# One layer of a hybrid diffusion trunk: the gated output weights prepared earlier and kept in scratch, the router's column sums moved, eight weight splits on another engine

## The chip, the cores and the metric

The kernel runs on one core of a Trainium2 chip. Its engines run side by side and each works through its own queue in order: TensorE (PE for matmuls, PEld for the loading of their weights), VectorE (DVE), ScalarE (ACT), GpSimd (POOL) and SyncE (SP), which here only starts transfers. ACT and POOL start transfers too. Sixteen DMA engines carry them all between the chip's main memory and SBUF, the memory on the core. The metric is the device time of one execution in microseconds (us), as the median of the runs.

## The reference

One layer with 2048 latent tokens and 256 context tokens of width 1024. Four token mixers of width 256 (HGRN2, gated DeltaNet, a grouped Fourier transform, Mamba-2 SSD) read the normed input `hl`. Their outputs are merged and projected, and a mixture of 16 experts follows:

```python
def merge_branches(h, outs, w_gate, b_gate, w_branch, w_out):
    t = [jax.nn.sigmoid(h @ w_gate[g] + b_gate[g]) * (outs[g].astype(h.dtype) @ w_branch[g])
         for g in range(N_BRANCH)]
    return (t[0] + t[1] + t[2] + t[3]) @ w_out

xl = post_norm(DEEPNORM_ALPHA * xl + g1_l * y_l, ln1_g[l], ln1_b[l])
hl2 = modulate(xl, sh2_l, sc2_l)
xl = post_norm(DEEPNORM_ALPHA * xl + g2_l * expert_choice_ffn(hl2, w_router[l], ...), ln2_g[l], ln2_b[l])
```

`g1_l`, `sh2_l`, `sc2_l` and `g2_l` are rows of 1024 numbers worked out from the conditioning vector. The router computes softmax(`hl2 @ w_router`), and each expert takes the 256 tokens that like it most.

## The kernel before, in words

A matmul in float32 is made of three in a shorter format: `split` (lines 105 to 108) makes a high part `hi` with a cast on ACT and a low part `lo` with a subtraction, on DVE or, where `eng` says so, on POOL. `mm3` (lines 110 to 117) then issues high x high (line 115), high x low (116) and low x high (117). So L106 is always the cast, L108 the subtraction and L115 to L117 the three matmuls, and the names of the tiles tell which work it is.

The stages in order of time: projections of the input (to about 800 us), gated DeltaNet (its chain ends with `finish`, whose last store of `d_oB` goes out at 1519.7 us), HGRN, which takes its four heads one after the other from inside the DeltaNet stretch to 1726 us, SSD, the Fourier mixer (to 2068 us), the merge, routing (about 2570 to 2650 us) and the experts (to the end). From 800 to 2143 us TensorE also works through `gates`, the products of the input with `w_gate`: 2 groups of tokens by 32 blocks of 128 columns. The framework's planner puts them between the other stages' matmuls when it fixes every engine's order at compile time, by the order of the program and its own estimates. On the chip that order doesn't change: an engine whose next instruction has to wait stands still. A tile with `bufs=n` has n buffers in turn, and the load into the next one waits in its queue until that buffer is free.

HGRN (`hgrn`, lines 829 to 939) loads its inputs from POOL's queue. After heads 1 and 3 it calls `finish` (lines 941 to 962): sums of squares, a normalisation, then four times a load of 512 columns of a gate (`fns`, one buffer, from SP, line 959), two DVE operations (960, 961) and a store from SP (962). `hoT`, the tile that is finished, has one buffer, so head 2 may write its outputs (line 936) only once all four stores of head 0 and 1 have landed.

The merge works on groups of 512 tokens in the order 2, 3, 0, 1. `branch` (lines 1644 to 1678) does one mixer n of one group i: it loads the mixer's output `bo` and splits it, gets the weights `bwh` and `bwl` for each pair of 128-column blocks, does six matmuls for each block, and DVE multiplies the result by the gate `bt` that it loads from `d_th` (1674, 1676); the sum into `t` (1677) is on DVE for group 2 and on POOL for the others. The weights come from `w_branch` through a split for all four mixers of group 2 and for the last two (n = 2, 3) of group 3; that split's subtraction is on POOL. The first two mixers' parts go to the scratch `d_wbs` in group 2 and the last two's in group 3, from ACT's queue (1663); the other passes read them back from SP (1666). Group 2's `branch` runs beside the last blocks of `gates`.

`combine` (lines 1685 to 1710) starts with `out_weights`, four calls of two blocks each: it loads the row g1 (`oa`), then each of the 8 blocks `ox` (128x1024, three buffers) of `w_out`, multiplies it by 0.5 g1 on DVE (1724) and splits it into `owh` and `owl`. The first call also loads and scales the router's weights (`router_weights`: 128 values of `wrt`, and `wrc`, a transfer of 2048 single numbers), the last one loads four rows of 1024 and calls `router_sums`, which sums the router's columns on DVE (1749), adds them over the partitions with a matmul (1750) and copies the result (1751). Then group 3's `branch` alternates with `out_proj` of the group before: four tiles of 128 tokens, each a split of `t` into `oth`, `otl`, 48 matmuls, two layer norms on DVE with a square root on ACT (`rst`, L288), and stores; and with `logits`, eight transposes, a copy by ACT (`oxT`, L1802) and eight small matmuls (1805).

Of the kernel before, what the change touches and what calls it, by code (L numbers as in the profile page):

```python
# [9 lines left out]
F32 = mybir.dt.float32  # L10
F32R = mybir.dt.float32r
# [4 lines left out]
OP = mybir.AluOpType  # L16
# [3 lines left out]
D = 1024  # L20
NB = D // 128
SEQ = 2048
CTX = 256
TOT = CTX + SEQ
W = 256
# [17 lines left out]
def ap(t, offset, dims):  # L43
    return bass.AP(tensor=t.tensor, offset=t.offset + offset, ap=[list(d) for d in dims])


class Kernel:
# [522 lines left out]
    def front(self):  # L570
        nc, tc = self.nc, self.tc
        self.pos_c = self.const([128, D // 2], F32, "pos_c")
        for j in range(2):
            nc.sync.dma_start(self.pos_c[j * 64:(j + 1) * 64], self.a["pos_cc"])
        with tc.tile_pool(name="wp", bufs=1, reuse_waits="tile") as self.wp, tc.tile_pool(name="mc", bufs=1) as self.cpool:
            with tc.tile_pool(name="hp", bufs=1, reuse_waits="tile") as self.hp:
                with tc.tile_pool(name="ha", bufs=1, reuse_waits="tile") as hap, self.psum(4, 4):
                    self.stage_z(hap)
                with self.psum(3, 3):
                    with tc.tile_pool(name="hg", bufs=1, reuse_waits="tile") as p:  # L580
                        self.head_sel(p)
                        with tc.tile_pool(name="g3", bufs=1, reuse_waits="tile") as q:
                            self.gdn_merge(q)
                        with tc.tile_pool(name="g4", bufs=1, reuse_waits="tile") as q:
                            self.gdn_chain(q, p)
                        sp = tc.tile_pool(name="sp", bufs=1, reuse_waits="tile", side="right")
                        spp = sp.__enter__()
                        self.hgrn(p)
                        self.ssd_early(spp)
                    with tc.tile_pool(name="mp", bufs=1, reuse_waits="tile") as p:  # L590
                        self.ssd(p)
                    sp.__exit__(None, None, None)
                    with tc.tile_pool(name="mp", bufs=1, reuse_waits="tile") as p:
                        self.fourier(p)
                    self.cq = tc.tile_pool(name="cq", bufs=1, reuse_waits="tile", side="right")
                    self.cp = self.cq.__enter__()
                    self.merged = self.cp.tile([128, NB, 512], F32, name="t", bufs=2)
                    first = chain.from_iterable(self.branch(self.cp, 2, n, self.merged) for n in range(4))
                    self.gates(first)
                    for _ in first:  # L600
                        pass
            self.cpool = self.cn
# [338 lines left out]
    def finish(self, p, o, b, norm, gate, out, eps=EPS):  # L941

        nc = self.nc
        w = p.tile([128, 1], F32, name="fnw", bufs=2)
        nc.sync.dma_start(w, ap(self.a[norm], 128 * b, [[1, 128], [1, 1]]), allow_slow_non_contiguous=True)

        def tmp():
            return p.tile([128, 512], F32, name="fns", bufs=1)

        def sq(_, c, n):  # L950
            q = tmp()
            nc.scalar.activation(q, o[:, c:c + n], AF.Square)
            return q
        rs = self.head_rs(p, sq, [[(c, 512) for c in range(0, SEQ, 512)]], 1.0 / 64, self.hind, eps)
        rs = self.head_parts(p, rs)
        for g in range(4):
            s = slice(g * 512, g * 512 + 512)
            gt = tmp()
            nc.sync.dma_start(gt, ap(self.dram(gate, (W, SEQ)), 128 * b * SEQ + g * 512, [[SEQ, 128], [1, 512]]))
            nc.vector.tensor_mul(o[:, s], o[:, s], self.head_bc(rs, 4 * g, 512))  # L960
            nc.vector.scalar_tensor_tensor(o[:, s], o[:, s], w, gt, op0=OP.mult, op1=OP.mult)
            nc.sync.dma_start(ap(self.dram(out, (W, SEQ)), 128 * b * SEQ + g * 512, [[SEQ, 128], [1, 512]]), o[:, s])

# [678 lines left out]
    def branch(self, p, i, n, acc):  # L1644

        nc = self.nc
        g, name = ((2, "oC"), (3, "oD"), (0, "oA"), (1, "oB"))[n]
        o = p.tile([128, 2, 512], F32, name="bo", bufs=1)
# [5 lines left out]
        for b in range(NB):  # L1654
            if b % 2 == 0:
                wh, wl = [p.tile([128, 2, 256], F32R, name="bw" + s, bufs=3) for s in "hl"]
                parts = [(t.rearrange("p k c -> p (k c)").bitcast(F32), kept[j, 4 * g + b // 2]) for j, t in enumerate((wh, wl))]
                if i == 2 or i == 3 and n > 1:
                    wr = p.tile([128, 2, 256], F32, name="bw", bufs=3)
                    nc.sync.dma_start(wr, ap(self.a["w_branch"], g * W * D + b * 128, [[D, 128], [128 * D, 2], [1, 256]]))  # L1660
                    self.split(wr, wh, wl, nc.gpsimd)
                    for t, k in parts if i == 3 or n < 2 else ():
                        nc.scalar.dma_start(k, t)
                else:
                    for t, k in parts:
                        nc.sync.dma_start(t, k)
            ps = self.big()
            s = slice(b % 2 * 128, b % 2 * 128 + 128)
# [16 lines left out]
    def combine(self, p, op, rc):  # L1685

        nc = self.nc
        self.op = op
        for n in range(4):
            self.out_weights(op, n)  # L1690
        old, last = self.merged, 2
        xs = []

# [3 lines left out]
        for i in (3, 0, 1):  # L1697
            t = p.tile([128, NB, 512], F32, name="t", bufs=2)
# [10 lines left out]
            route()  # L1709
        self.logits(p, *xs[0])  # L1710

    def out_weights(self, p, n):

        nc = self.nc
        modr = self.dram("modr", (4, D))
        if n == 0:
            self.g1 = p.tile([128, D], F32, name="oa", bufs=1)
            nc.sync.dma_start(self.g1, ap(modr, 0, [[0, 128], [1, D]]))
            self.router_weights(p)
            self.wo = [p.tile([128, NB, D], F32R, name="ow" + s) for s in "hl"]  # L1720
        for k in (2 * n, 2 * n + 1):
            r = p.tile([128, D], F32, name="ox", bufs=3)
            nc.sync.dma_start(r, ap(self.a["w_out"], k * 128 * D, [[D, 128], [1, D]]))
            nc.vector.scalar_tensor_tensor(r, r, 0.5, self.g1, op0=OP.mult, op1=OP.mult)
            self.split(r, self.wo[0][:, k], self.wo[1][:, k])
        if n == 3:
            self.rowt = [self.row_tile(p, n, t, o) for n, t, o in (("sh2", modr, D), ("sc2", modr, 2 * D),
                                                                   ("lg", self.a["ln1_g"], 0), ("lb", self.a["ln1_b"], 0))]
            self.router_sums(p)

    def router_weights(self, p):

# [568 lines left out]
```

## Time and profile before

| | us |
|---|---|
| median of 3 runs | 3817.27 (3816.72 to 3832.19) |
| the profiled execution | 3813.39 |
| its span, first to last instruction | 3811.4 |
| TensorE busy in the span | 3516.1 |

The mean granted TensorE clock is 0.957 of full speed. In the slices of the span TensorE is nearly full in the experts' stage (2650 to 3550 us) and mostly between 8 and 10 tenths before it. The lowest slices are around the start of `combine` (2150 to 2200 us) and in routing (2550 to 2650 us). Times below are microseconds from the span's start unless marked ns; in a row of a timeline the first number is the start, the second the length, and the bracket tells how long the engine was idle before and what ended it.

### The profile page before, as it was taken

To read this page: it belongs to the slowest core of one execution; us is meant where nothing else is said; L and a number is where in the kernel's file an instruction comes from. 1 tells how busy PE (TensorE), PEld (TensorE's weight loads), DVE (VectorE), ACT (ScalarE), POOL (GpSimd) and SP (SyncE) were. 2 spreads that over 40 slices of the span, in tenths; PEclk is the share of its full clock that TensorE was granted. 3 is DMA by queue.
4 is the path that set the end of the run, shared out by engine and by line. 5 is a ranking of instruction groups with operands and counts; after the bars stand their busy time and mean duration, and the time that the engine had idled before them with its cause. 6 is when DMAs were issued, how large, how long until landed. Compare 5 with 4: busy or idle time off the path is not lost. (4 is left out here: it accounts for less than half of the span.)

```text
span 3811.4 us, 60074 instructions
## 1 busy us (share of the span) xinstructions
PE 3516.1 (92%) x23429; PEld 2939.9 (77%) x23429; DVE 2399.4 (63%) x4455; ACT 1222.9 (32%) x1863; POOL 785.0 (21%) x577
## 2 busy tenths in 40 slices
PE   5999999999888999898899789994999999999997
PEld 3897778777666667677777677873999999999887
DVE  6528762257557778567864666776555555555788
ACT  3513232212334223232234211112444444444342
POOL 2100013321222111214422254453101001001011
PEclk8999999999899999898999989996999999999999
DMA  7544438764656566424456787743666666657786
GB/s 237 166 143 133 145 96 196 182 170 130 154 123 152 169 186 200 124 66 138 135 172 216 237 272 233 252 149 134 205 206 199 220 209 212 217 193 222 270 274 206
DMA packets 602061, 699.81 MB, mean 184 GB/s; under 512 B 153809, under 2 KB 460465, under 8 KB 598577
## 3 DMA queue, kind: packets, MB, share of 16 engines
q1 hardware_dynamic: 537776, 547.56, 46.9%
q0 software_dynamic: 24800, 90.71, 8.9%
q10 hardware_dynamic: 39200, 57.69, 4.3%
q8 instruction: 185, 3.03, 0.3%
q14 instruction: 100, 0.81, 0.1%
HBM read 525.37 MB, written 170.45 MB: 183 GB/s over the span
## 5 line engine op out<-in xcount | busy, mean ns | idle before, releaser
L115 PE MATMUL big<-h2h,whi 128*128 128x512 f32 x704 | 292.5, 416 | 4.6 <-ACT ev L1595 4.6
L115 PE MATMUL mx<-exh,wgateh 128*128 128x256 f32 x1024 | 294.9, 288 | 0.0
L117 PE MATMUL big<-h2h,wlo 128*128 128x512 f32 x704 | 291.8, 415 | 1.4 <-POOL wlo L108 1.4
L116 PE MATMUL big<-h2l,whi 128*128 128x512 f32 x704 | 291.1, 413 | 0.0
L116 PE MATMUL mx<-exl,wgateh 128*128 128x256 f32 x1024 | 289.8, 283 | 0.0
L116 PE MATMUL mx<-exl,wuph 128*128 128x256 f32 x1024 | 289.8, 283 | 0.0
L115 PE MATMUL mx<-exh,wuph 128*128 128x256 f32 x1024 | 289.8, 283 | 0.0
L117 PE MATMUL mx<-exh,wupl 128*128 128x256 f32 x1024 | 289.8, 283 | 0.0
L117 PE MATMUL mx<-exh,wgatel 128*128 128x256 f32 x1024 | 289.8, 283 | 0.0
L116 PE MATMUL big<-h3l,whi 128*128 128x512 f32 x704 | 287.6, 408 | 0.0
L115 PE MATMUL big<-h3h,whi 128*128 128x512 f32 x704 | 287.5, 408 | 0.0
L117 PE MATMUL big<-h3h,wlo 128*128 128x512 f32 x704 | 286.1, 406 | 0.0
L108 POOL TENSOR_TENSOR wlo<-wraw,whi 128x1024 fp32r<-128x1024 f32 x60 | 147.4, 2457 | 643.0 <-ACT whi L106 611.7
L2126 POOL DMA_INDIRECT d_acc<-ey,ix x30 | 52.2, 1739 | 874.7 <-DVE ey L2119 837.4
L117 PE MATMUL big<-wdh,hidl 128*128 128x512 f32 x496 | 195.1, 393 | 10.5 <-DVE hidl L108 10.5
L108 DVE TENSOR_TENSOR wdl<-wdr,wdh 128x1024 fp32r<-128x1024 f32 x124 | 150.9, 1217 | 82.4 <-ACT wdh L106 82.3
L116 PEld LDWEIGHTS mx<-exl,wgateh 128*128 128x128 f32 x1024 | 196.3, 192 | 2.7 <-DVE exl L108 0.3
L115 PEld LDWEIGHTS mx<-exh,wgateh 128*128 128x128 f32 x1024 | 196.1, 192 | 2.4
L116 PEld LDWEIGHTS mx<-exl,wuph 128*128 128x128 f32 x1024 | 196.6, 192 | 0.0
L117 PEld LDWEIGHTS mx<-exh,wupl 128*128 128x128 f32 x1024 | 196.6, 192 | 0.0
L115 PEld LDWEIGHTS mx<-exh,wuph 128*128 128x128 f32 x1024 | 196.6, 192 | 0.0
L115 PE MATMUL big<-wdh,hidh 128*128 128x512 f32 x496 | 196.0, 395 | 0.2 <-ACT hidh L106 0.2
(642 smaller groups left out, 9127.4 us busy)
## 6 DMA issues: line engine op xcount, KB each, us to landing
wgr<-in_w_ff_gate_dram SPq DMA_DIRECT2D x64, 1024.0 KB
wgr<-in_w_ff_up_dram SPq DMA_DIRECT2D x64, 1024.0 KB
wdr<-in_w_ff_down_dram SPq DMA_DIRECT2D x128, 512.0 KB
wraw<-in_w_gate_dram POOLq DMA_DIRECT2D x64, 512.0 KB, 5.1
d_th<-ev ACTq DMA_DIRECT2D x128, 256.0 KB
bt<-d_th SPq DMA_DIRECT2D x128, 256.0 KB
adr<-in_ada_w_dram SPq DMA_DIRECT2D x128, 128.0 KB
bwh<-d_wbs SPq DMA_DIRECT2D x40, 256.0 KB
```

The source lines that it names most:

```text
L108: return (eng or self.nc.vector).tensor_tensor(lo, src, hi, op=OP.subtract)
L115: self.nc.tensor.matmul(ps, wh, xh, start=first and k == 0, stop=False)
L116: self.nc.tensor.matmul(ps, wh, xl, start=False, stop=False)
L117: self.at_pe = self.nc.tensor.matmul(ps, wl, xh, start=False, stop=last and k == n - 1).ins
L2126: nc.gpsimd.indirect_dma_start(out=acc, out_offset=bass.IndirectOffsetOnAxis(ap=ix[e][:, k:k + 1], axis=0), in_=weighted(e, k), in_offset= ...
```

## The change

Six edits in one.

- `scaled_out`, new, runs between DeltaNet and HGRN in the program's order: it loads the row g1 in two halves and `w_out` in 16 pieces of 128x512, multiplies each by 0.5 g1 on DVE and stores it to a new scratch `d_wos`. `issue_after(self.fin)` puts its transfers behind the last store of DeltaNet's `finish` in SP's queue; `finish` now keeps that store in `self.fin`. Its tiles have two buffers (`wor`) and one (`wog`).
- `out_weights` loads the 8 blocks from `d_wos` and only splits them; the row `oa` and the multiplication are gone.
- `router_weights` and `router_sums` are called ahead of group 2's `branch` and the last blocks of `gates`, in the pool of the merge.
- In `branch` the subtraction of the weights' split goes to DVE in group 3; in group 2 it stays on POOL.
- The four calls of `out_weights` are one.
- The memory kept for POOL's DMA descriptors is set to 8192 bytes.

```diff
                             self.gdn_chain(q, p)
+                        with tc.issue_after(self.fin):
+                            self.scaled_out()
...
                     self.cp = self.cq.__enter__()
+                    self.router_weights(self.cp)
+                    self.router_sums(self.cp)
                     self.merged = self.cp.tile([128, NB, 512], F32, name="t", bufs=2)
...
-                    self.split(wr, wh, wl, nc.gpsimd)
+                    self.split(wr, wh, wl, nc.gpsimd if i == 2 else None)
...
-        for n in range(4):
-            self.out_weights(op, n)
+        self.out_weights(op)
...
+    def scaled_out(self):
+        nc, p = self.nc, self.wp
+        wos = self.dram("wos", (D, D))
+        for j in range(2):
+            g = p.tile([128, 512], F32, name="wog", bufs=1)
+            nc.sync.dma_start(g, ap(self.dram("modr", (4, D)), j * 512, [[0, 128], [1, 512]]))
+            for k in range(NB):
+                r = p.tile([128, 512], F32, name="wor", bufs=2)
+                at = k * 128 * D + j * 512, [[D, 128], [1, 512]]
+                nc.sync.dma_start(r, ap(self.a["w_out"], *at))
+                nc.vector.scalar_tensor_tensor(r, r, 0.5, g, op0=OP.mult, op1=OP.mult)
+                nc.sync.dma_start(ap(wos, *at), r)
...
+    def out_weights(self, p):
...
+        for k in range(NB):
             r = p.tile([128, D], F32, name="ox", bufs=3)
-            nc.sync.dma_start(r, ap(self.a["w_out"], k * 128 * D, [[D, 128], [1, D]]))
-            nc.vector.scalar_tensor_tensor(r, r, 0.5, self.g1, op0=OP.mult, op1=OP.mult)
+            nc.sync.dma_start(r, ap(wos, k * 128 * D, [[D, 128], [1, D]]))
             self.split(r, self.wo[0][:, k], self.wo[1][:, k])
...
-    nc = bacc.Bacc("TRN2", target_bir_lowering=False, num_devices=1)
+    nc = bacc.Bacc("TRN2", target_bir_lowering=False, num_devices=1, dynamic_dma_scratch_size=8192)
```

## Rows read from the trace of the kernel before

**Rows 1.** The page's first part: busy us (share of the span) xinstructions of each engine.
```profile
PE 3516.1 (92%) x23429; PEld 2939.9 (77%) x23429; DVE 2399.4 (63%) x4455; ACT 1222.9 (32%) x1863; POOL 785.0 (21%) x577
```

**Rows 2.** Windows: stretch, length, busy us of each engine (xinstructions), TensorE's clock, DMA share, GB/s.
```profile
2150.00:2200.00 50.00, 26.50 (x97) 18.72 (x96) 45.82 (x59) 13.29 (x15) 6.66 (x5) 0.80 0.85 264
```

**Rows 3.** Timeline of TensorE, 2173 to 2200 us.
```profile
2187.54 0.64 PE L1750 MATMUL mx<-wrs,ones 128*128 128x32 f32 x2 [14.16 <-DVE wrs L1749]
2193.08 0.76 PE L115 MATMUL big<-boh,bwh 128*128 128x512 f32 x1 [4.90 <-DMA bwh<-d_wbs]
...
2197.91 0.63 PE L117 MATMUL big<-boh,bwl 128*128 128x512 f32 x1
...
2199.46 0.40 PE L116 MATMUL big<-bol,bwh 128*128 128x512 f32 x1
2199.69 0.39 PE L115 MATMUL big<-boh,bwh 128*128 128x512 f32 x1
```

**Rows 4.** Groups by line, 2140 to 2210 us: count, busy us, mean ns, idle before.
```profile
L1724 DVE SCALAR_TENSOR_TENSOR ox<-ox,oa 128x1024 f32<-128x1024 f32 x8 | 9.7, 1219 | 0.4 <-DMA ox<-in_w_out_dram 0.4
L1749 DVE TENSOR_REDUCE wrs<-wrt 128x16 f32<-128x128 f32 x1 | 0.4, 359 | 0.0
```

**Rows 5.** Timeline of SP's queue, 2178 to 2188 us (starts of transfers).
```profile
2178.51 0.43 SPq L1649 DMA_DIRECT2D bo<-d_oC  x1
2183.56 4.01 SPq L1723 DMA_DIRECT2D ox<-in_w_out_dram  x3
```

**Rows 6.** Windows around the stall, behind it, and in HGRN (columns as in rows 2).
```profile
2145.00:2205.00 60.00, 36.41 (x139) 26.65 (x138) 54.46 (x71) 16.04 (x18) 9.79 (x17) 0.83 0.85 265
...
2221.00:2300.00 79.00, 70.55 (x287) 56.80 (x287) 52.53 (x89) 14.00 (x24) 57.64 (x37) 0.87 0.72 234
2245.00:2257.00 12.00, 9.92 (x32) 8.53 (x33) 5.34 (x11) 3.80 (x6) 3.75 (x4) 0.57 0.97 327
...
1540.00:1580.00 40.00, 33.09 (x216) 28.16 (x214) 6.56 (x8) 7.45 (x12) 9.94 (x9) 0.87 0.52 135
```

**Rows 7.** DMA traffic of the core, 2157 to 2167 us, in 40 slices of 0.25 us.
```profile
GB/s 352 303 295 303 283 156 86 74 147 172 213 156 188 164 262 254 222 215 105 42 24 4 1 1 156 188 131 82 106 164 188 295 369 418 467 369 385 393 402 402
```

**Rows 8.** Waits, 2157 to 2300 us (TensorE), 2225 to 2330 (ACT), 2140 to 2330 (SP): total us, times, longest.
```profile
PE mx L1805 <- ACT oxT L1802: 7.3, 2, 4.1
...
ACT bwh L106 <- POOL bwl L108: 7.4, 1, 7.4
...
ACT oth L106 <- POOL bwl L108: 3.1, 1, 3.1
...
SPq L1671 <- POOL t L1677: 49.1, 20, 7.9
```

**Rows 9.** Groups of 2221 to 2300 us, and DVE's L1677 on `bt`, 2160 to 2230 (ns min/median/max).
```profile
L108 POOL TENSOR_TENSOR bwl<-bw,bwh 128x512 fp32r<-128x512 f32 x8 | 11.4, 1422 | 3.9 <-ACT bwh L106 3.9
...
L1677 DVE TENSOR_TENSOR t<-t,bt x11: 661/683/1778, 2160.2 to 2180.6; 128x512 f32<-128x512 f32 x11
```

**Rows 10.** HGRN's `finish` of heads 0 and 1: timelines of DVE, POOL and SP.
```profile
1545.74 2.42 DVE L961 SCALAR_TENSOR_TENSOR hoT<-hoT,fnw,fns 128x512 f32<-128x512 f32 x1 [3.10 <-DMA fns<-d_ag]
...
1559.57 0.75 DVE L961 SCALAR_TENSOR_TENSOR hoT<-hoT,fnw,fns 128x512 f32<-128x512 f32 x1 [4.50 <-DMA fns<-d_ag]
...
1545.21 2.40 POOL L108 TENSOR_TENSOR wlo<-wraw,whi 128x1024 fp32r<-128x1024 f32 x1 [25.86 <-ACT whi L106]
...
1555.51 0.38 SPq L959 DMA_DIRECT2D fns<-d_ag  x1
1560.35 0.32 SPq L962 DMA_DIRECT2D d_oA<-hoT  x1
```

**Rows 11.** Who waited in HGRN, 1515 to 1570 us (SP: 1540 to 1760), and ACT's next step.
```profile
PE two L934 <- ACT hoT L936: 6.8, 1, 6.8
...
SPq L959 <- PE mx L208: 144.4, 1, 144.4
...
1564.55 1.07 ACT L936 ACTIVATE hoT<-two 64x512 f32<-64x512 f32 x2 [7.69 <-DMA d_oA<-hoT]
```

More of the change, by code (lines that the diff above doesn't have):

```diff
@@ L961, in finish @@
             nc.vector.scalar_tensor_tensor(o[:, s], o[:, s], w, gt, op0=OP.mult, op1=OP.mult)
-            nc.sync.dma_start(ap(self.dram(out, (W, SEQ)), 128 * b * SEQ + g * 512, [[SEQ, 128], [1, 512]]), o[:, s])
+            self.fin = nc.sync.dma_start(ap(self.dram(out, (W, SEQ)), 128 * b * SEQ + g * 512, [[SEQ, 128], [1, 512]]), o[:, s]).ins
     def tri_masks(self, p):
@@ L1710, in combine @@
         self.logits(p, *xs[0])
-    def out_weights(self, p, n):
-        nc = self.nc
[L1715 to L1721, printed above, removed]
+    def scaled_out(self):
[11 more added lines that the diff above has]
+    def out_weights(self, p):
+        nc = self.nc
+        modr, wos = self.dram("modr", (4, D)), self.dram("wos", (D, D))
+        self.wo = [p.tile([128, NB, D], F32R, name="ow" + s) for s in "hl"]
+        for k in range(NB):
             r = p.tile([128, D], F32, name="ox", bufs=3)
-            nc.sync.dma_start(r, ap(self.a["w_out"], k * 128 * D, [[D, 128], [1, D]]))
-            nc.vector.scalar_tensor_tensor(r, r, 0.5, self.g1, op0=OP.mult, op1=OP.mult)
+            nc.sync.dma_start(r, ap(wos, k * 128 * D, [[D, 128], [1, D]]))
             self.split(r, self.wo[0][:, k], self.wo[1][:, k])
[L1726 to L1729, printed above, removed]
+        self.rowt = [self.row_tile(p, n, t, o) for n, t, o in (("sh2", modr, D), ("sc2", modr, 2 * D),
+                                                               ("lg", self.a["ln1_g"], 0), ("lb", self.a["ln1_b"], 0))]
     def router_weights(self, p):
```

## The prediction

> **What bounds the kernel now.** I read the page's first part, the windows in order of time, then timelines and waits where a window is low. TensorE is busy 3516 us of 3811, DVE 63% [rows 1], so the end moves mainly by idle time of TensorE and by its clock. The chain that ended last is followed only through scattered pieces of the experts' stage, which the change leaves alone, so I work from the stages. The poorest 50 us outside routing are the start of `combine`: TensorE works 26.5 us of them, DVE 45.8, and the DMA engines are busy 85% of the time [rows 2]. TensorE stops at 2173.4 us (14.16 before 2187.54), runs the router's matmul, waits 4.9 us more for `bwh`, and resumes at 2193.08: 19.7 us from stop to restart [rows 3]. It then runs at the lower clock, 1.2 GHz instead of 2.4: the next twelve matmuls, to 2197.91, start 0.44 us apart, those from 2199.46 on 0.23. That costs 12 x 0.2 = 2.4 us more [rows 3], so the whole stall is worth 22 us.
>
> Why it stands: the reductions behind the router's matmul (L1749) sit in DVE's queue among the multiplications (L1724) and splits of the output weights. SP is held up by the same loop: its fifth `ox` load waits for a buffer that a split must free, until 2183.56, and the first `bwh` load stands behind three `ox` loads whose issue takes until 2187.57 [rows 5]. So one stall has three parents: DVE, SP's order and the DMA engines.
>
> **The change, part by part.** The sum is made against the profiled execution, 3813.4 us (span 3811.4 and 2.0 around it), which is 3.9 under the median, 3817.3; the difference is carried over to the median.
>
> *The start of `combine`.* Gone from it are eight multiplications of 1.219 us, 9.75 us of DVE, and two reductions of 0.36: 10.5 us together [rows 4]. From 2145 to 2205 DVE was busy 54.5 us of 60, so nearly every one of these microseconds delayed something. The DMA engines give a second bound: busy 0.85 of the 60 us, 51 us, so the stretch can't shrink by more than 9 us plus the transfers that leave it [rows 6]. Those are the row `oa`, 512 KB, some 1.7 us (265 GB/s at 0.85 of the engines make 312 for all of them), and `wrc`, whose 2048 single numbers press the traffic to 105, 42, 24, 4, 1 and 1 GB/s in six slices of 0.25 us, 1 to 2 us [rows 7]. That allows 12 to 13 us. The loads of `w_out` themselves stay, now from `d_wos`. Ends: 0 (the wait passes whole to `bwh` or to the DMA engines) and -22 (all of the stall and its clock). I take -11, where DVE's and the DMA engines' accounts meet. What is late next: `bo` and the first `bwh`, both on SP, behind the remaining `ox` loads and four rows of 512 KB.
>
> *The eight splits of group 3.* From 2221 to 2300 us POOL is busy 57.6 of 79 us, DVE 52.5 [rows 6]. The splits take POOL 1.422 us each, 11.4 in all; on DVE an operation of the same shape has a median of 0.683, so DVE gets 8 x 0.68 = 5.5 us and has 26 idle [rows 6, 9]. Behind POOL queue ACT (7.4 and 3.1 us for `bwl`, as its store of `bwl` is in ACT's queue) and SP, 49.1 us in 20 waits for the sum in `t` that frees `bt` [rows 8]. TensorE pays in two places: 7.3 us of waiting for `oxT`, which ACT makes after what held it [rows 8], and the lower clock afterwards. The window 2245 to 2257 has a clock of 0.57, which on 9.9 us of work is about 4 us, and the second place is like it. So some 15 us hang on this loop, but only the first of the two waits stands directly behind a late `bwl`; before the second ACT waited for a `bo` that SP issued late. Ends: +5.5 (DVE's own time, all exposed) and -15. I take -6: the first place and its clock mostly gone, the second shorter.
>
> DVE and POOL also slow each other: L961 took 2.42 us while POOL's 2.40 us split ran, 0.75 alone [rows 10]. The Trainium skill (SBUF — State Buffer, Who interferes with whom) has a rule for it: an instruction of VectorE with two SBUF inputs and a GpSimd one that reads SBUF take an exclusive lock in turn. The row agrees, and by the rule each split taken off POOL also frees up to one such wait of DVE: up to 8 x 1.4 = 11 us, which would put this part near its far end. It speaks against the next part: a multiplication that meets POOL's split takes 1.7 us more, and as POOL was busy a quarter of the 40 us in HGRN [rows 6], 16 x 0.25 x 1.7 = 7 us of DVE come on top there.
>
> *`scaled_out` in HGRN.* It adds 16 multiplications of 128x512; L961 has that shape and takes 0.75 us [rows 10]: 12 us of DVE. It adds 34 transfers, 32 of 256 KB and two half rows of 256 KB: 8.9 MB, at 312 GB/s 29 us of the DMA engines. Cover: from 1540 to 1580 us DVE is busy 6.6 of 40 us and the DMA engines 52%, so 33 and 19 us are free [rows 6], and SP then stands 144 us before its next load [rows 11]. But the neighbour is a chain that counts: `finish` of heads 0 and 1 sends its stores and loads through SP up to 1560.35, ACT may write `hoT` again at 1564.55, and TensorE stands 6.8 us for that [rows 10, 11]. What is queued behind a waiting instruction of `scaled_out`: on SP the loads of `fns` and the stores of `hoT`, on DVE the steps of HGRN's scan. The order is fixed by the planner, which knows of the added work and can put matmuls of `gates` into the gap; not covered is what the chip takes longer than planned. Ends: 0 and +12 (every multiplication on the chain). I take +3, four multiplications.
>
> *The router's part, earlier.* Five small DVE operations, two loads and one matmul now stand at the end of the Fourier stage, where `gates` gives TensorE work. `wrc` can hold up a load there by 2 us or so [rows 7]. Ends 0 and +3; I take 0, since TensorE's work there doesn't hang on these loads; without `gates` it would cost the whole wait.
>
> *POOL's descriptor memory and the merged calls.* In no view did POOL wait for room for descriptors, so I take 0. No row bounds it from above; it is left to the range.
>
> Sum: -11 - 6 + 3 = -14: 3799.4 against the profiled execution, 3803 as a median.
>
> **The rivals.**
>
> *Everything goes, -34.* The stall with its clock (-22) and both waits for `oxT` with theirs (-15), +3: 3783. For it: one loop of DVE, SP and POOL feeds all three, and it loses work on all of them. Against: the DMA engines were busy 85% of these 60 us [rows 6], and nearly all of the bytes stay.
>
> *The stall changes its name, -1.* The router's matmul is gone from there, but `bo` and `bwh` still land at 2190 because rows and `ox` loads go first in SP's queue: the first part gives 3, the second 1, HGRN takes 3: 3816. For it: the last 4.9 us of the stall were already a wait for `bwh` [rows 3], and the DMA share is high. Against: three `ox` loads stood before that `bwh` only because their buffers came free late [rows 5].
>
> *SP's queue in HGRN makes it slower, +19.* `scaled_out` is earlier in the program than HGRN's `finish`, and with two buffers its third load waits until the first store has landed. One round for two pieces is a load (1555.51 to 1559.57, 4.1 us), a multiplication (0.75) and a store (1560.35 to 1564.55, 4.2 us) [rows 10, 11]: 9.0 us, eight rounds 72 us. Each round that the planner puts ahead of `finish`'s loads of `fns`, and that takes longer on the chip than planned, holds up `finish`, `hoT` and heads 2 and 3, and TensorE stands in order behind them. Two such rounds eat the 17 us that the rest brings; from four on (+36) the kernel is slower by 19: 3836. For it: the place is a stall already, and SP is strictly in order. Against: after 1560 SP is empty for 144 us, room for all eight rounds, and what the planner foresees is filled with `gates`.
>
> **How the numbers follow.** The forecast, with its own range 3790 to 3813, 0.50; everything goes 0.22; another name 0.16; slower 0.12. 0.5%, about what a measurement of this kernel can tell from no change, is 19 us: 3798 and 3836. Faster by more: all of the second case but a little, 0.20, and a third of the first, 0.17: 0.37. Slower by more: 0.08 of the last case's 0.12. Same: 0.55. The range, 3780 to 3832, takes in the first rival and most of the last one's smaller forms, and leaves out about 0.1 on each side. The time is the forecast's, 3803.
>
> **What would show it.** Right: no wait of TensorE for `wrs` near 2170 us; DVE under 46 us of 60 at the start of `combine`; the stall 5 to 12 us and ended by `bwh` or `bo`; POOL under 48 of 79 us in group 3 and ACT not waiting for POOL's `bwl`; between 1520 and 1600 us, TensorE's wait for `hoT` longer by no more than 5 us. Wrong: a stall of 18 us under another name (second rival), a stall under 3 us together with no wait for `oxT` (first), a wait of 15 us or more in HGRN (third), or the time moving in the experts' stage, which nothing here foresees.

## The result and the profile after

The changed kernel takes 3854.15 us (median of 5 runs, 3845.33 to 3863.20) beside 3817.27 of the kernel before (3808.44 to 3832.19): 1.0086 times as long, 95% interval 1.0063 to 1.0108. Forecast were 3803 us and a range of 3780 to 3832. The kernel got slower, by 37 us between the medians and by 33 us by the ratio, beyond the range and to the other side.

The spans differ by 41.0 us (3852.4 and 3811.4). The first part of the page after, which answers to [rows 1]:

```profile
PE 3537.1 (92%) x23429; PEld 2957.9 (77%) x23429; DVE 2404.2 (62%) x4471; ACT 1221.7 (32%) x1863; POOL 780.6 (20%) x569
```

TensorE does the same matmuls but is busy 21 us longer, as its clock is lower (0.951 instead of 0.957); the other 20 us are idle time. To see where, I cut both spans at the last start of a stage's last store or step, as the tile views give it: `d_oB` (end of DeltaNet), `d_oA` (HGRN), `d_oD` (SSD), `d_oC` (Fourier), `d_th` (gates), and ACT's last `oxT` (merge). All numbers are lengths in us, the first is a point of time.

| kernel | last d_oB | HGRN | SSD | Fourier | gates' end | merge |
|---|---|---|---|---|---|---|
| before | 1519.7 | 206.3 | 222.8 | 119.4 | 75.8 | 441.0 |
| after | 1523.9 | 226.9 | 227.6 | 125.7 | 78.8 | 440.3 |
| e7 (nearly the order of before) | 1518.5 | 204.2 | 227.0 | 124.3 | 76.3 | 441.7 |

Half of the loss is HGRN: +20.6. The merge, where 17 us were to be won, is the same. SSD, Fourier and the gates' end add 14 us, but e7 below, whose engines have the very order of the kernel before in these stages, shows 9 us of the same in SSD and Fourier. So profiles of one order differ by so much, and from their lengths I charge those stages with nothing.

The length has another weakness: the planner can put matmuls of `gates` into a stage or take them out. From the last `d_oB` to the last `d_th` TensorE works through the same 3255 to 3257 matmuls in all kernels here, so its idle time in this stretch (length less busy time) can be compared directly. Windows (columns as in [rows 2]) of the kernel before, then of the kernel after, with its Fourier stretch:

```profile
1519.70:2144.00 624.30, 566.76 (x3255) 454.63 (x3256) 376.30 (x735) 196.71 (x343) 176.82 (x127) 0.94 0.48 148
```
```profile
1523.90:2182.90 659.00, 583.79 (x3256) 467.86 (x3257) 387.19 (x756) 195.88 (x343) 176.61 (x127) 0.91 0.50 154
1978.40:2104.10 125.70, 112.94 (x548) 89.65 (x547) 67.87 (x91) 55.72 (x90) 20.63 (x15) 0.97 0.56 179
```

TensorE is idle 57.5 us of it before and 75.2 after (53.6 in e7). Of the 17.7 more, 9.8 are in HGRN (below) and 5.5 in Fourier, where 12.8 us are idle instead of 7.3 (e7: 8.3) and TensorE has some ten matmuls fewer.

**HGRN.** First the windows of the kernel before (columns as in [rows 2]): from the last `d_oB` to the last `d_oA`, and the Fourier stretch.

```profile
1519.70:1726.00 206.30, 185.96 (x1379) 147.32 (x1380) 113.92 (x300) 68.06 (x125) 38.48 (x29) 0.93 0.32 98
...
1948.80:2068.20 119.40, 112.13 (x557) 89.37 (x556) 64.48 (x88) 55.91 (x91) 16.59 (x11) 1.00 0.56 186
```

Then those of the kernel after: HGRN, the 40 us that answer to the last row of [rows 6], two pieces of HGRN, the start of `combine` and group 3 (the first and second row of [rows 6]).

```profile
1523.90:1750.80 226.90, 196.76 (x1402) 155.76 (x1403) 127.42 (x316) 68.60 (x126) 38.39 (x29) 0.90 0.43 132
1540.00:1580.00 40.00, 36.02 (x242) 30.06 (x241) 14.70 (x30) 7.34 (x12) 9.90 (x9) 0.87 0.73 218
1570.00:1600.00 30.00, 23.14 (x161) 18.48 (x159) 6.74 (x11) 6.57 (x12) 6.80 (x8) 0.98 0.86 229
1600.00:1650.00 50.00, 39.51 (x319) 29.31 (x320) 37.27 (x87) 17.39 (x35) 8.78 (x8) 0.81 0.30 101
2190.00:2250.00 60.00, 38.05 (x145) 28.20 (x144) 42.12 (x67) 14.75 (x16) 8.40 (x7) 0.83 0.85 284
2259.00:2338.00 79.00, 67.36 (x287) 53.86 (x286) 59.01 (x100) 12.68 (x22) 48.13 (x29) 0.91 0.73 238
```

Of HGRN's 20.6 us, TensorE is busy in 10.8 (196.8 instead of 186.0) and idle in 9.8. Some 6 of the 10.8 are 23 more matmuls of `gates` that the new order has in this stretch (514 instead of 491, 0.27 us each); the rest goes with the clock, 0.90 instead of 0.93. The 40 us in which I had looked for cover are better than before: TensorE works 36.0 instead of 33.1. The hole comes behind them. Timelines of DVE, ACT, SP and TensorE after (start, length, and in the bracket the idle time before and what ended it):

```profile
1569.39 1.28 DVE L1726 SCALAR_TENSOR_TENSOR wor<-wor,wog 128x512 f32<-128x512 f32 x2
1582.12 3.36 DVE L1726 SCALAR_TENSOR_TENSOR wor<-wor,wog 128x512 f32<-128x512 f32 x2 [11.45 <-DMA wor<-in_w_out_dram]
1596.22 0.69 DVE L1726 SCALAR_TENSOR_TENSOR wor<-wor,wog 128x512 f32<-128x512 f32 x1 [10.74 <-DMA wor<-in_w_out_dram]
1597.84 0.69 DVE L1726 SCALAR_TENSOR_TENSOR wor<-wor,wog 128x512 f32<-128x512 f32 x1 [0.92 <-DMA wor<-in_w_out_dram]
1598.45 1.84 DVE L927 SCALAR_TENSOR_TENSOR hS<-hS,hPc 64x64 f32<-64x64 f32 x6
```
```profile
1586.08 0.78 ACT L922 ACTIVATE hS<-two 64x256 f32<-64x256 f32 x2 [3.66 <-PE two L919]
```
```profile
1575.67 1.03 SPq L1725 DMA_DIRECT2D wor<-in_w_out_dram  x2
1584.91 0.93 SPq L1727 DMA_DIRECT2D d_wos<-wor  x2
1593.57 1.84 SPq L1725 DMA_DIRECT2D wor<-in_w_out_dram  x2
```
```profile
1606.05 1.12 PE L877 MATMUL two<-hqz,hk 128*64 128x64 f32 x16 [11.51 <-ACT hqz L899]
```

All 16 multiplications as a group, 1520 to 1620 us (count, busy us, mean ns, idle before):

```profile
L1726 DVE SCALAR_TENSOR_TENSOR wor<-wor,wog 128x512 f32<-128x512 f32 x16 | 14.5, 920 | 34.0 <-DMA wor<-in_w_out_dram 33.9
```

From 1570.7 to 1596.2 DVE does two multiplications and waits 22.2 us for `wor`. ACT writes `hS`, on which the next scan steps (L927) work, at 1586.08, and DVE begins them at 1598.45, as they stand in its order behind two more multiplications. In the kernel before DVE begins 0.4 us behind ACT:

```profile
1579.72 0.78 ACT L918 ACTIVATE hS<-two 64x256 f32<-64x256 f32 x2 [4.41 <-PE two L915]
1580.13 4.02 DVE L923 SCALAR_TENSOR_TENSOR hS<-hS,hPc 64x64 f32<-64x64 f32 x6 [19.81 <-ACT hS L918]
```

So the scan is some 12 us late. TensorE then waits 11.5 us for the next scores' input (until 1606.05) and has a clock of 0.81 in the 50 us from 1600 (the same 50 us of the kernel before: 0.93).

**The start of `combine`.** TensorE, SP and ACT after, answering to [rows 3] and [rows 5]:

```profile
2213.79 0.40 PE L117 MATMUL big<-boh,bwl 128*128 128x512 f32 x1
2230.49 1.22 PE L115 MATMUL big<-boh,bwh 128*128 128x512 f32 x2 [16.31 <-ACT boh L106]
...
2236.61 0.58 PE L116 MATMUL big<-bol,bwh 128*128 128x512 f32 x1
2237.03 0.40 PE L117 MATMUL big<-boh,bwl 128*128 128x512 f32 x1
```
```profile
2216.41 4.51 SPq L1736 DMA_DIRECT2D ox<-d_wos  x2
2220.98 0.42 SPq L1686 DMA_DIRECT2D row_lg<-in_ln_g_dram  x1
2221.45 0.42 SPq L1686 DMA_DIRECT2D row_lb<-in_ln_b_dram  x1
2221.92 0.43 SPq L1653 DMA_DIRECT2D bo<-d_oC  x1
```
```profile
2229.38 1.06 ACT L106 ACTIVATE boh<-bo 128x1024 fp32r<-128x1024 f32 x1 [3.52 <-DMA bo<-d_oC]
```

The router's matmul is gone from here and DVE is busy 42.1 of 60 us instead of 54.5, but TensorE stands 16.3 us instead of 19.7 and again runs at 1.2 GHz behind it (starts 0.43 us apart up to 2236.61, then 0.23). SP issues `bo` behind eight `ox` loads and four rows, so it lands at 2229. The DMA engines' share is 0.85, as before.

**Group 3.** POOL is busy 48.1 of 79 us instead of 57.6, and no wait of ACT for POOL's `bwl` is left. Waits of 2225 to 2340 us (SP: 2180 to 2370), answering to [rows 8]:

```profile
PE mx L1815 <- ACT oxT L1812: 5.5, 2, 5.0
...
PE big L115 <- DVE bt L1680: 3.2, 2, 2.8
...
PE big L117 <- DVE bwl L108: 1.4, 1, 1.4
...
SPq L1675 <- POOL t L1681: 49.0, 21, 8.1
```

The wait for `oxT` shrinks by 1.8 us, while `bt` and `bwl`, which DVE now makes later, cost 4.6 (before, 0.2). TensorE is busy 67.4 of 79 us, in the row of before 70.6.

### The profile page after: what moved, and what is told of

It is laid out like the page before. It is cut to its first block, busy times and chain, and to the rows that moved or that the text cites. A ratio compares the mean times of both kernels' runs of the same rounds, so it can differ in the third digit from the quotient of the medians.

```text
span 3852.4 us, 60163 instructions
## 1 busy us (share of the span) xinstructions
PE 3537.1 (92%) x23429; PEld 2957.9 (77%) x23429; DVE 2404.2 (62%) x4471; ACT 1221.7 (32%) x1863; POOL 780.6 (20%) x569
## 5 line engine op out<-in xcount | busy, mean ns | idle before, releaser
L117 PEld LDWEIGHTS mx<-exh,wgatel 128*128 128x128 f32 x1024 | 197.0, 192 | 0.0
```

What stands on the lines that cost most here:

```text
L117: self.at_pe = self.nc.tensor.matmul(ps, wl, xh, start=False, stop=last and k == n - 1).ins
```

## The experiments

My theory after this: DVE's multiplications wait in order for late `wor` loads and hold up the scan. The first rival, A: SP's queue and the DMA engines hold up HGRN. The second, B: the planner's new order, which the router's move alone could bring. Ratios are to the kernel before, on the same chip, with a 95% interval; lengths are cut as in the table above.

**Which part is it?** Four kernels.

```diff
  e1: the kernel after
-                        with tc.issue_after(self.fin):
-                            self.scaled_out()
...                      (out_weights loads w_out and multiplies by 0.5 g1 again)
  e2: the kernel before
+                        with tc.issue_after(self.fin):
+                            self.scaled_out()
...                      (out_weights loads d_wos; 8192 bytes for POOL's descriptors)
  e3: the kernel after, in scaled_out
-                nc.vector.scalar_tensor_tensor(r, r, 0.5, g, op0=OP.mult, op1=OP.mult)
  e5: the kernel before
+                    self.router_weights(self.cp)
+                    self.router_sums(self.cp)
...                      (and both calls gone from out_weights)
```

> The changed kernel without scaled_out: the output weights are loaded from w_out and multiplied by 0.5 g1 at the start of combine, as before; the router's part is early and group 3's splits are on DVE, as after. Theory (the loss comes from scaled_out in HGRN, where its multiplications stand in order on DVE and wait for late wor loads): last store of d_oB to last store of d_oA 206 us as before (207), not 227; last store of gate products at 2143 +-6; combine's start still about 55 us; time 3800 to 3820. Rival A (SP's queue and the DMA engines' load in HGRN, also from scaled_out): the same here. Rival B (the router's part ahead of the last gate blocks, or the new order that the planner makes because of it): time 3840 to 3855.

> The kernel before with scaled_out alone (and the small descriptor memory that makes room for its tiles): combine reads d_wos and doesn't multiply; the router's part stays in combine and group 3's splits on POOL. Theory and rival A: HGRN 220 to 230 us between the last stores of d_oB and d_oA, the last gate product after 2170, time 3840 to 3860. Rival B: HGRN as before (206), time 3800 to 3820.

> The changed kernel with the 16 multiplications of scaled_out left out (w_out goes to d_wos unscaled, so y lacks the factor 0.5 g1); all 34 transfers stay, in nearly the same order on SP. Theory (DVE's multiplications wait in order and hold up the scan's steps): HGRN back to 206 to 212 us between the last stores of d_oB and d_oA, time 3812 to 3828. Rival A (SP's queue holds up the loads of fns and the stores of hoT, and the DMA engines are crowded): HGRN still 220 us or more, time 3842 to 3856.

> The kernel before with router_weights and router_sums alone moved ahead of group 2's branch and the last gate blocks. Theory and rival A: HGRN 206 us, last gate product 2143 +-6, no wait of TensorE for wrs at the start of combine, time 3800 to 3820. Rival B: last gate product after 2165, time 3835 to 3855.

| kernel | ratio | last d_oB | HGRN | SSD | Fourier | gates' end | merge |
|---|---|---|---|---|---|---|---|
| e1 | 1.0019 (1.0002 to 1.0036) | 1527.7 | 207.3 | 223.7 | 121.4 | 79.4 | 442.0 |
| e2 | 1.0087 (1.0064 to 1.0109) | 1522.4 | 228.0 | 228.6 | 125.8 | 78.9 | 446.6 |
| e3 | 1.0012 (0.9993 to 1.0031) | 1524.4 | 211.3 | 228.4 | 122.5 | 74.3 | 440.2 |
| e5 | 1.0006 (0.9989 to 1.0023) | 1526.0 | 201.7 | 224.4 | 120.2 | 76.9 | 442.2 |

`scaled_out` alone gives the whole loss (e2), without it HGRN is as before (e1, e5). So the router's move is not the cause. B stays in the form that `scaled_out` itself brings a new order; I come back to it with g2. With all transfers but no multiplications HGRN costs 5 us (e3), and TensorE's idle time to the last `d_th` is 58.4 us, as before. So the 8.9 MB by themselves cost little, and so far that speaks for the theory against A.

**Is it DVE?** In f3 POOL multiplies; in h3 DVE multiplies, but only the row, so that it doesn't wait for the loads of `w_out`; h4 has four buffers.

```diff
  f3: the kernel after, in scaled_out (g halved once by POOL)
-                nc.vector.scalar_tensor_tensor(r, r, 0.5, g, op0=OP.mult, op1=OP.mult)
+                nc.gpsimd.tensor_tensor(r, r, g, op=OP.mult)
  h3: the kernel after, in scaled_out (4096 bytes for POOL's descriptors)
-                nc.vector.scalar_tensor_tensor(r, r, 0.5, g, op0=OP.mult, op1=OP.mult)
+                r = p.tile([128, 512], F32, name="wos", bufs=2)
+                nc.vector.scalar_tensor_tensor(r, g, 0.5, g, op0=OP.mult, op1=OP.mult)
  h4: the kernel after, in scaled_out (4096 bytes for POOL's descriptors)
-                r = p.tile([128, 512], F32, name="wor", bufs=2)
+                r = p.tile([128, 512], F32, name="wor", bufs=4)
```

> The changed kernel with scaled_out's 16 multiplications on POOL (a tensor_tensor by a half of g1 that is made once for each half row). Theory (the cost in HGRN is DVE's order: work that waits for late loads stands ahead of the scan's steps): POOL can wait without harm, HGRN 208 to 214 us between the last stores of d_oB and d_oA instead of 227, ratio 1.001 to 1.004. Rival A (SP's queue and the DMA engines): HGRN 220 or more, ratio 1.006 and more. Rival C (the multiplications' own time, wherever they run, through the memory that DVE and POOL share): HGRN 216 to 222, ratio 1.004 to 1.007.

> The changed kernel with the 16 multiplications of scaled_out on the row alone (g times 0.5 g into a tile of its own, which is stored), so that DVE has the same work but doesn't wait for the loads of w_out; loads and stores stay (d_wos doesn't hold the weights, so y is wrong; POOL's descriptor memory is 4096 bytes to make room for the tile). Theory (DVE's in-order waits for late loads, 34 us in the changed kernel): HGRN 206 to 214 us, ratio 1.000 to 1.003. Rival A (SP's queue, or the DMA engines): 218 or more, ratio 1.005 and more.

> The changed kernel with four buffers for wor instead of two (and 4096 bytes of descriptor memory for the room): four rounds instead of eight, and all of them ahead of finish's second load of fns in SP's queue. Theory: the rounds are over before head 3's scan, DVE's waits for wor fall under 20 us and stand where no scan step is due; HGRN 210 to 217, ratio 1.002 to 1.005. Rival A (finish held up in SP's queue): head 0 and 1's last store of d_oA 55 us or more after d_oB's last store (46 in the changed kernel, 41 before), TensorE waits for hoT, HGRN 222 or more.

| kernel | ratio | last d_oB | HGRN | merge |
|---|---|---|---|---|
| f3 | 1.0056 (1.0040 to 1.0072) | 1527.0 | 229.0 | 438.9 |
| h3 | 1.0065 (1.0037 to 1.0092) | 1531.4 | 227.2 | 438.3 |
| h4 | 1.0103 (1.0076 to 1.0131) | 1536.5 | 228.7 | 439.2 |

All three contradict the theory in its narrow form: HGRN stays at 227 to 229 with DVE's wait for `wor` gone (f3, h3) or cut from 33.9 to 13.3 us (h4). (In h3 DVE still waits 9.4 us, in eight times, for the stores that free its two `wos` buffers.) Timelines of SP, ACT and TensorE's longest wait in h3:

```profile
1581.71 0.79 SPq L963 DMA_DIRECT2D fns<-d_ag  x1
1584.23 3.10 SPq L1728 DMA_DIRECT2D d_wos<-wos  x2
1587.43 1.43 SPq L1725 DMA_DIRECT2D wor<-in_w_out_dram  x2
1588.91 0.75 SPq L966 DMA_DIRECT2D d_oA<-hoT  x1
```
```profile
1596.92 1.07 ACT L940 ACTIVATE hoT<-two 64x512 f32<-64x512 f32 x2 [12.46 <-DMA d_oA<-hoT]
```
```profile
PE two L938 <- ACT hoT L940: 11.8, 1, 11.8
```

Here all eight turns go through SP among the transfers of `finish`, the last store of head 0 and 1 goes out at 1588.91, 57.5 us behind the last `d_oB` (before: 1560.35 - 1519.7 = 40.7), and head 2 may write `hoT` at 1596.9, 65.5 behind it (before 44.9). Followed further, the timelines show where each kernel falls behind. Starts in us behind the last `d_oB`: the last store of heads 0 and 1, ACT's next steps into `hoT` and `hS`, the first `hqz` and `hkT` after them, the stage's last store; then TensorE's idle time to the last `d_th`.

| kernel | `d_oA`, heads 0 and 1 | `hoT` | `hS` | `hqz` | `hkT` | last `d_oA` | idle to `d_th` |
|---|---|---|---|---|---|---|---|
| before | 40.7 | 44.9 | 60.1 | 68.0 | 84.5 | 206.3 | 57.5 |
| after | 45.6 | 47.8 | 62.2 | 81.2 | 101.2 | 226.9 | 75.2 |
| e3 | 47.5 | 51.0 | 65.7 | 72.3 | 90.0 | 211.3 | 58.4 |
| f3 | 51.5 | 56.2 | 72.0 | 80.5 | 107.6 | 229.0 | 69.4 |
| h3 | 57.5 | 65.5 | 80.1 | 88.0 | 104.6 | 227.2 | 71.2 |
| h4 | 66.4 | 68.6 | 82.9 | 89.6 | 107.2 | 228.7 | 72.2 |

The kernel after loses 13 us up to `hqz`, where DVE stands in the turns, and 17 up to `hkT`; 4 more come in the `finish` of heads 2 and 3, which no turn meets, and I did not trace them. h3 and h4 have their whole loss (20.6 and 23.7 us) at `hoT`, behind `finish`, and keep it to the end. TensorE fills much of it with matmuls of `gates` (1431 and 1460 matmuls in HGRN, before 1379), but these are then missing later: TensorE's idle time grows by 14 and 15 us up to the last `d_th`. f3 loses 11 us at `hoT`, as SP waits for POOL, and 11 more between `hqz` and `hkT`. Waits, then POOL, TensorE and DVE in that second piece:

```profile
PE two L938 <- ACT hoT L940: 9.7, 1, 9.7
...
SPq L1728 <- POOL wor L1727: 50.9, 16, 7.7
```
```profile
1604.69 1.25 POOL L1727 TENSOR_TENSOR wor<-wor,wog 128x512 f32<-128x512 f32 x1 [8.36 <-DMA wor<-in_w_out_dram]
...
1609.19 2.35 POOL L108 TENSOR_TENSOR wlo<-wraw,whi 128x1024 fp32r<-128x1024 f32 x1
```
```profile
1611.60 0.79 PE L117 MATMUL big<-h2h,wlo 128*128 128x512 f32 x1 [4.84 <-POOL wlo L108]
```
```profile
1607.99 3.85 DVE L903 TENSOR_TENSOR hQ<-hQ,hf 64x256 f32<-64x256 f32 x2 [0.50 <-ACT hqz L899]
...
1617.29 4.78 DVE L903 TENSOR_TENSOR hQ<-hQ,hP 64x256 f32<-64x256 f32 x2
```

POOL waits 8.4 us for a `wor` load, the split `wlo` of the gates' weights stands behind two multiplications, and TensorE waits 4.8 us for it. Beside POOL's multiplications and splits two pairs of DVE's L903 take 3.85 and 4.78 us; other pairs take 0.87. So rival C has a part in f3, some 7 us of DVE's time.

In the kernel after head 2's write comes at 1571.74, 47.8 behind, and is held by nothing of `finish`; there DVE is the way. So both were right, each in its own kernels, as the traces show it: a turn of `scaled_out` (load, multiplication, store) stands in two queues that HGRN's chain uses, and what is made lighter in one is paid in the other.

**Out of HGRN.** f1 and f2 call the first two parts of group 3 ahead of `out_weights` (for the start of `combine`, below); g1 and g2 are f1 with `scaled_out` wholly on POOL (queue and arithmetic), or called between SSD and Fourier.

```diff
  f1 (kernel after), f2 (kernel before): combine
-        self.out_weights(op)                             (f2: its four calls)
...
                 for _ in self.branch(p, i, n, t):
                     pass
-                xs.append((4 * last + n, *self.out_proj(p, 4 * last + n, old)))
-                route()
+                if i == 3 and n < 1:
+                    continue
+                if i == 3 and n == 1:
+                    self.out_weights(op)                 (f2: its four calls)
+                for m in range(n + 1) if i == 3 and n == 1 else (n,):
+                    xs.append((4 * last + m, *self.out_proj(p, 4 * last + m, old)))
+                    route()
  g2: f1, in front
+                    with tc.issue_after(self.fin):     (fin: SSD's last store)
+                        self.scaled_out()
                     with tc.tile_pool(name="mp", bufs=1, reuse_waits="tile") as p:
                         self.fourier(p)
```

> The changed kernel with the first two parts (n = 0, 1) of group 3's branch called ahead of out_weights, and the first two out_proj after it. Theory of combine's start (TensorE stands because SP issues bo and the first weights of group 3 behind the ox loads and the rows, so the work taken off DVE there changes nothing): the 17 us stall goes, the first out_proj finds owh ready behind 96 matmuls; 10 to 20 us less than the changed kernel, 1.003 to 1.006 times the kernel before. Rival (the DMA engines, busy 0.8 to 1.0 there, carry the same bytes and set the length of the stretch): the wait moves to owh or bwh, at most 3 us less, 1.008 and more.

> The kernel before with the same new order at combine's start and nothing else; out_weights still multiplies by 0.5 g1. Theory: 8 to 18 us faster than the kernel before, ratio 0.995 to 0.998. Rival: 0.999 to 1.001.

> f1 (the changed kernel with the parts first) with the whole of scaled_out on POOL: its loads, its multiplications and its stores, so that no instruction of it stands in DVE's or SP's queue. Theory, widened after f3 (the chain load, multiplication, store turns with two buffers in the queues that the HGRN chain uses: in the changed kernel DVE waits in it, in f3 SP waits 51 us for POOL's results): HGRN 206 to 213 us between the last stores of d_oB and d_oA, against 228 in f1 and 229 in f3; ratio to the kernel before 0.996 to 0.9995 (f1: 1.003). Rival A2 (the 8.9 MB crowd the DMA engines): HGRN 220 or more, 1.002 and more.

> f1 with scaled_out called between SSD and the Fourier mixer, behind SSD's last store, with the same engines (loads and stores on SP, multiplications on DVE). The order of the other work through HGRN stays nearly that of f1. Theory: HGRN 206 to 211 us; the Fourier stretch (last d_oD to last d_oC), where DVE is busy a half of the time and no chain hangs on SP, 119 to 127; ratio 0.994 to 0.999. Rival (the new order of the planner, not the waits, makes HGRN longer): HGRN 220 or more, ratio 1.002 and more.

| kernel | ratio | last d_oB | HGRN | Fourier | merge |
|---|---|---|---|---|---|
| f1 | 1.0030 (1.0013 to 1.0046) | 1529.2 | 228.2 | 125.1 | 428.6 |
| f2 | 1.0011 (0.9990 to 1.0031) | 1523.8 | 205.0 | 120.1 | 447.8 |
| g1 | 1.0047 (1.0023 to 1.0072) | 1566.1 | 205.2 | 120.1 | 432.6 |
| g2 | 0.9989 (0.9963 to 1.0015) | 1521.9 | 206.1 | 146.5 | 427.9 |

In g2 HGRN is as before. But the order of TensorE and DVE there is, against my expectation, not that of f1: all 1379 and 299 instructions stand as in the kernel before, while of f1's order TensorE's has 1047 in common. So g2 doesn't part the waits from the order, and no run has the changed kernel's order in HGRN without its waits. Against an order that costs by itself speaks e3: its order on TensorE is even further from that of before (878 in common), and it loses 5 us. And the price moves along: Fourier takes 27 us more, of which TensorE is idle 10.8 and busy 16.8, with 36 more matmuls and a clock of 0.94. Its window and its wait of DVE:

```profile
1951.00:2098.00 147.00, 128.91 (x593) 101.95 (x592) 74.33 (x105) 57.15 (x92) 21.07 (x12) 0.94 0.68 219
```
```profile
DVE wor L1730 <- DMA wor<-in_w_out_dram: 22.8, 8, 6.9
```

g1 is a miss as a test: `issue_after` did not hold POOL's queue, the planner put `scaled_out` into the projections, and the last `d_oB` is 37 us later than in f1 (1566.1 and 1529.2); why so much I did not follow. The view of the tile `wor`, line L1731 (ns min/median/max, first and last start):

```profile
L1731 POOL TENSOR_TENSOR wor<-wor,wog x16: 1252/1297/5861, 268.0 to 362.5; 128x512 f32<-128x512 f32 x16
```

So whether `scaled_out` on POOL inside HGRN would be free was not tried.

The start of `combine`: with the parts first, TensorE's long wait is gone in f1; its longest there is 4.09 us, and the 60 us that begin 8 us behind the last gate product have 46.6 busy instead of 38.1 (windows, then TensorE):

```profile
2196.00:2256.00 60.00, 46.61 (x185) 35.02 (x186) 42.64 (x72) 11.23 (x14) 15.98 (x12) 0.97 0.84 276
```
```profile
2222.89 0.50 PE L115 MATMUL big<-boh,bwh 128*128 128x512 f32 x1 [4.09 <-DVE bt L1680]
```

The merge is shorter by 12 us in f1 and g2 and by 8 in g1. So the order of work set the stall, at about the same DMA share. With the multiplications still in `combine` the long stall goes too: in f2 the longest wait there is 2.84 us, and the 60 us that answer to these have 49.7 busy. Yet the merge doesn't get shorter in f2 (447.8): waits of 2 to 4 us, for `bwl`, `bt` and `oxT`, come in the 200 us behind instead. In g4, below, it is shorter by 5. So ending the stall paid in full only in the changed kernel, where DVE is freed as well, and freeing DVE alone (the kernel after) paid nothing.

**The other parts.** e6 has group 3's splits on DVE alone (run twice), g4 is e6 with f2's order, i1 is e5 and e6 together, e7 has only the smaller descriptor memory. h2 is e6 with the multiplications of `out_weights` on POOL, h1 is g4 with the same.

```diff
  e6, g4, i1, h1, h2
-                    self.split(wr, wh, wl, nc.gpsimd)
+                    self.split(wr, wh, wl, nc.gpsimd if i == 2 else None)
  e7
-    nc = bacc.Bacc("TRN2", target_bir_lowering=False, num_devices=1)
+    nc = bacc.Bacc("TRN2", target_bir_lowering=False, num_devices=1, dynamic_dma_scratch_size=8192)
  h1, h2: out_weights (g1 halved once by POOL)
-            nc.vector.scalar_tensor_tensor(r, r, 0.5, self.g1, op0=OP.mult, op1=OP.mult)
+            nc.gpsimd.tensor_tensor(r, r, self.g1, op=OP.mult)
```

> The kernel before with group 3's eight splits on DVE alone. The prediction's -6 (ends +5.5 and -15): ratio 0.996 to 1.0014; POOL under 48 of 79 us from 2221 to 2300, no wait of ACT for POOL's bwl, the wait for oxT shorter than 7.3 us. Since the stretch from the first out_proj to the last logits took 440 us in both kernels, I now expect nothing: 0.999 to 1.001.

> The kernel of e6 once more (the kernel before with group 3's eight splits on DVE alone), in more rounds: it is the best so far. If its gain is real: ratio 0.996 to 0.9985 again; if e6 was luck: 0.999 to 1.001.

> The kernel before with group 3's splits on DVE and the first two parts of group 3 ahead of out_weights; no scaled_out, router as before. If the two gains add up as parts: e6 0.9973, f2 1.0011: 0.997 to 0.999. If the splits on POOL were what f2's later waits hung on: 0.993 to 0.997.

> The kernel before with the two parts of the change that cost nothing in HGRN: the router's part early and group 3's splits on DVE; no scaled_out, out_weights as before. If the parts add up (e5 1.0006, e6 0.9973): 0.997 to 0.9995. If e1 (1.0019, which has both, and one call of out_weights for four) shows that they don't: 1.000 to 1.003.

> The kernel before with 8192 bytes for POOL's DMA descriptors and nothing else; every engine's order is the same. The prediction's 0: ratio 0.999 to 1.001. Rival (POOL waits for room for descriptors in the experts' stage, where its indirect DMAs are): experts' stage 3 us or more longer, ratio above 1.0015.

> e6 (the kernel before with group 3's splits on DVE) with the eight multiplications of out_weights on POOL, which has nothing to do at combine's start, by a row that is halved once. No scaled_out. DVE loses 9.75 us where it is busy 54 of 60 us. If DVE sets the start of combine: ratio 0.992 to 0.996 (e6 0.9973). If the DMA engines and SP's order do (they are as before): 0.9965 to 0.998.

> The same with the first two parts of group 3 ahead of out_weights (the kernel g4 with out_weights' multiplications on POOL). In the changed kernel this order gained 11 us of combine once DVE was free of the multiplications (f1), in the kernel before nothing (f2, g4). So with DVE free of them: ratio 0.990 to 0.995; if the order needs the multiplications gone altogether, not only moved: 0.996 to 0.998.

| kernel | ratio | merge |
|---|---|---|
| e6, first and second time | 0.9973 (0.9957 to 0.9990), 0.9993 (0.9969 to 1.0017) | 443.3, 443.6 |
| g4 | 0.9976 (0.9955 to 0.9998) | 436.1 |
| i1 | 1.0008 (0.9988 to 1.0028) | 441.3 |
| e7 | 0.9999 (0.9977 to 1.0021) | 441.7 |
| h2 | 1.0022 (0.9993 to 1.0052) | 454.4 |
| h1 | 0.9995 (0.9971 to 1.0019) | 446.9 |

The splits on DVE gain nothing that stands up: the second run of e6 and i1 do not confirm the first, and the merge is not shorter. In e6 the wait for `oxT` is as long as before, 7.7 instead of 7.3 us, though POOL is relieved:

```profile
PE mx L1805 <- ACT oxT L1802: 7.7, 2, 4.4
```

The descriptor memory costs nothing (e7), the router's move neither (e5, i1). Taking the multiplications off DVE at `combine`'s start by giving them to POOL makes the merge 11 us longer (h2 against e6, h1 against g4); neither came out at either of its forecasts. No kernel here beats the one before by clearly more than two measurements of one kernel differ; g4 comes nearest, at 0.9976.

## Why the prediction was wrong

- **The step that failed is "`scaled_out` in HGRN: +3, ends 0 and +12".** HGRN grew by 20.6 us in the profile, by 21 to 23 in e2, f1, f3, h3 and h4; TensorE's idle time to the last `d_th` grew by 17.7. The far end, "every multiplication on the chain", priced the 16 multiplications by their own time; that came out nearly right, 14.5 us of DVE in all. It left out that DVE stands before a multiplication until its load has landed (33.9 us in all) and that everything behind it in order stands too. The idle 33 of 40 us of DVE [rows 6] were no cover: cover has to be free where the waiting instruction stands in the order, and there HGRN's scan was next.
- **The third rival was the right kind, in another queue.** It had the turns with two buffers and a chain held up behind them, and gave it 0.12 and 3836 us. It named SP alone. In the changed kernel `finish`'s last store is only 5 us later (1569.50 - 1523.9 = 45.6, before 40.7), and DVE is the place; in h3 and h4 SP is, as the rival said. A turn was also longer than its 9.0 us: from 1582.12 to 1596.22, 14.1. The load issued at 1575.67 was used at 1582.12, 6.4 us instead of 4.1; the next load waited from the store at 1584.91 to 1593.57, 8.7 instead of 4.2. The DMA engines were busy 0.86 of the time then, 0.52 in the row of before; that this made the transfers longer is likely, but no run took other transfers away.
- **The start of `combine`, -11, became 0.** Right: no wait for `wrs`, DVE under 46 of 60 us. Wrong: the stall of 5 to 12 us was 16.3, under another name. It is the second rival's picture, `bo` late behind rows and `ox` loads. I had held against it that the `ox` loads waited only for DVE; but the last two still went out at 2216.41, and f1 and f2 show that the order of the work was the thing, though only f1's merge is shorter for it.
- **The splits, -6, became nothing** that can be measured. Right: POOL at 48.1 of 79 us, where under 48 had been named, and no wait of ACT for POOL's `bwl`. Wrong: that TensorE's wait for `oxT` hung on it.
- **The router's part and the descriptor memory, 0:** right (e5 1.0006, e7 0.9999).
- **The lock between DVE and POOL:** two of the 16 multiplications met POOL's split and took 2.76 us (the first of the pair at 1582.12) and 2.33, the others 0.69 each: +3.7 in all where the row had made it 7, a term that the part's +3 didn't hold. The Trainium skill (SBUF — State Buffer, Who interferes with whom) says that an instruction of VectorE with two SBUF inputs and one of GpSimd that reads SBUF block each other; the trace agrees, at a small size here (f3, above, shows more of it).
- **How it follows:** -11, -6 and +3 were measured as 0, 0 and +21. Of the rest of the 41 us, 5.5 are new idle time of TensorE in Fourier, which no term had; what is left lies in stages whose length differs by up to 5 us between two profiles (e7), and is not told apart. By the ratio the loss is 33 us.

## What to carry to other kernels

Work that is moved into a hole costs what its engine waits for it, not what it computes: for each added instruction ask when its input lands, and what of the chain stands behind it in order. A load, an operation and a store in turns with few buffers put such waits into every queue that they pass, and taking one away can hand the price to the next. Where TensorE waits for a transfer at a stage's start, look at what is issued ahead of it: freeing the engine that also looked busy changed nothing here until the order was changed too. And where other work can be put into a stage, compare idle time over a stretch with the same work, not the stage's length.

## What the runs showed that I had not expected

- The same turns cost 21 to 23 us of HGRN in four makings (on DVE, on POOL, without DVE's wait for the loads, with four buffers), and 5 without the multiplications (e3). In TensorE's idle time to the last `d_th` that is 12 to 18 us and 1.
- TensorE pays twice for HGRN's late scan: 9.8 us idle, and then a clock of 0.81 in the 50 us that follow, where the kernel before has 0.93.
- POOL's 128x512 multiplication took 1.25 to 5.86 us in g1 (median 1.30); DVE's takes 0.69.
- Two measurements of one kernel in different sets of runs, e6, gave 0.9973 and 0.9993, with intervals that overlap: differences of 0.2% are not to be built on.
